# RWKV time mixing on one core: float32-word transpositions on TensorE between the matmuls of R, fewer units by the DMA crossbar

## The chip, the core and the metric

The kernel runs on one core of a Trainium2 chip. A core has TensorE (PE; its weight loads are listed as PEld), VectorE (DVE), ScalarE (ACT), GpSimd (POOL), SyncE (SP, which here only issues DMAs) and 16 DMA engines, each engine with a program of its own. The metric is the time of one execution on the device in microseconds (us), lower is better. The kernel before takes 199.12 us, the median of 3 runs (198.97 to 199.16).

## What is computed

`x` is 16 batches of 2048 tokens of 256 channels in float32. Each token is mixed with the one before it, multiplied by two 256 x 256 weights, gated, and multiplied by a third:

```python
x_prev[:, 1:, :] = x[:, :-1, :]          # zero for the first token
xv = x * time_mix_v + x_prev * (1 - time_mix_v)
xr = x * time_mix_r + x_prev * (1 - time_mix_r)
v = xv @ value_weight
r = xr @ receptance_weight
out = (1 / (1 + exp(-r)) * v) @ output_weight
```

(The reference also computes a `k`, which the output does not use.)

## The kernel before

**Tiles.** A unit is 512 tokens of one batch (`TU`), so there are 64 units, numbered `g` or `u`, four to a batch. TensorE needs the channels on the partitions, so each unit is transposed: tile `xt`, in two halves of 128 channels (`KO` = 2). The mix is written as xr = tm * (c * x_prev + x) with c = (1 - tm) / tm. The factor tm is multiplied into the weights once, at the start (`w_bf`), so a unit needs a scaling by `c_sb` (`scale`, `scale_pool` or `scale_act`, on DVE, POOL or ACT) and a sum (`add`, DVE), in tile `mix`.

**One step of the main loop** (over `g`) issues on TensorE: the four 512-column matmuls of R of unit g (`project`, into `psum_r`), the transpositions of a unit some six further on, the four matmuls of V of unit g (`psum_v`), and the eight 256-column matmuls of the output O of unit g - 1 (`out_matmuls`, `psum_o`). ACT takes the sigmoid of `psum_r` (`s_sb`), copies the transposed unit from PSUM (`ps_t`) to `xt`, and copies O to `o_sb`. DVE multiplies sigmoid and V (`z_sb`) and does the sums for the next units; POOL scales half of the pieces, each after a sum of DVE. From unit 10 on a piece for scaling holds two units. Which step scales and sums which unit is in the lists `products`, `sums`, `held` and `pooled`: the sum for R of unit g + 2 stands on DVE right behind z of step g.

**Two ways to transpose.** Units 0 to 39 (batches 0 to 9, `STAGED` = 10) are transposed by TensorE: x is loaded as bf16 (cast by the DMA), and eight 128 x 128 blocks are matmuls with x as the weights and the identity as the moving operand (`transposes`, `one`). Units 0 and 1, which come first, are loaded as float32 and transposed so. The last 24 units (batches 10 to 15) are cast into DRAM (`x_natural`) and brought in by two DMA transpositions through the crossbar (`by_dma`, issued by SP at steps 27 and 39, `T_AT`), three batches each. Steps from 34 on thus have no transpositions on TensorE; there ACT does some of the scaling (`FREE`), and O comes one step later (`LATE_O`).

**Queues.** SP issues the stores and the two crossbar transpositions in program order; stores of some steps are held back until a transposition has gone out (`FIRST`, `WAITING`). POOL issues the loads of x between its scalings (`LOADS` by unit to be transposed, `STAGE_AT` by step). A load for the second crossbar transposition waits in POOL's queue until the first has landed. The program order on every engine is written by hand, since the kernel schedules manually.

Names that the change touches: `transposes` and `one` (L254 on), `advance`, `project` (L384), `coefficients`, `first_transposes`, `scale`/`scale_pool`/`scale_act`, and the tables at the top. In the profile L272 is the transposition, L289 its copy by ACT, L384 the matmuls of R and V, L416 those of O, L376 the sums, L711 z, L672 the sigmoid, L364 the scaling by POOL, L254 the crossbar.

Of the kernel before, what the change touches and what calls it, by code (L numbers as in the profile page):

```python
# [1 line left out]

# [6 lines left out]
FP32 = mybir.dt.float32  # L9
# [6 lines left out]
def kernel(  # L16
# [39 lines left out]
    STAGED = 10  # L56
# [14 lines left out]
    SPARE = 9 * UB // 2  # L71
# [13 lines left out]
        (5, 0): (8, 10),  # L85
        (6, 0): (9,),
        (7, 0): (11,),
        (7, 1): (12,),
# [5 lines left out]
    xtpool = ctx.enter_context(tc.tile_pool(name="xtpool", bufs=2))  # L94
# [70 lines left out]
    tm_rows = consts.tile([2 * KO, P], FP32)  # L165
    w_f32 = consts.tile([P, 2, KO, D], FP32)
    for m, tm in enumerate([time_mix_r, time_mix_v]):
        nc.scalar.dma_start(
            out=tm_rows[m * KO : (m + 1) * KO, :], in_=tm.rearrange("(ko p) -> ko p", p=P)
        )  # L170

    def load_halves(e):
# [8 lines left out]
        out=w_f32[:, 0], in_=receptance_weight.rearrange("(ko p) n -> p ko n", p=P)  # L181
    )
    load_halves(1)
    nc.sync.dma_start(out=w_f32[:, 1], in_=value_weight.rearrange("(ko p) n -> p ko n", p=P))
# [47 lines left out]
    tm_prev = consts.tile([P, 2, KO], FP32)  # L232

    def coefficients():
        ps = ps_o_pool.tile([P, 2, KO], FP32, name="psum_o")
        nc.tensor.transpose(
            out=ps.rearrange("p m k -> p (m k)"), in_=tm_rows, identity=ident_f[: 2 * KO, : 2 * KO]
        )
# [21 lines left out]
    def transposes(i):  # L260

        b, e = divmod(i, UB)
        if b > 0 and e == 0:
            new_xt(b)
        if b >= BYUNIT:
            e = (e - 1) % UB
        j0 = 1 + e * UJ + (e if b < BYUNIT else 0)
        if b < BYUNIT or e == UB - 1:
            late_copies.append((b, e))

        def one(ps, jj, ko, src, idn):
            nc.tensor.transpose(  # L272
                out=ps[:, jj], in_=src[:, jj, ko * P : (ko + 1) * P], identity=idn
            )
# [14 lines left out]
        nc.scalar.copy(out=xt[b][:, j0 : j0 + UJ], in_=ps)  # L289
        if i in SHIFT_ACT:  # L290
            j, n = (j0 - 1, UJ) if b < BYUNIT else (0, J)
            nc.scalar.copy(out=xt[b][:, j, :, 1:P], in_=xt[b][:, j + n, :, 0 : P - 1])
            shifted.append((b, e))

    def first_transposes():
        def part(lo, n, pool, name):
            ps = pool.tile([P, n, KO, P], FP32, name=name)
            for jj in range(n):
                for ko in range(KO):
                    nc.tensor.transpose(  # L300
                        out=ps[:, jj, ko],
                        in_=x_unit[:, 0, lo + jj, ko * P : (ko + 1) * P],
                        identity=ident_f,
                    )
# [7 lines left out]
        part(1, 1, ps_o_pool, "psum_o")  # L312

# [48 lines left out]
    def scale_pool(piece, after):
        b, m, _, _ = piece
        op = nc.gpsimd.tensor_scalar(  # L364
            out=mixed(piece, 1),
            in0=tokens(piece, 0, 1),
            scalar1=c_sb[:, m, 1:2],
            scalar2=1.0,
            op0=ALU.mult,
            op1=ALU.mult,  # L370
        )
        tc.add_manual_dep(op.ins, after.ins.name, SYNC, reason="one at a time")
# [7 lines left out]
    def project(ps, g, m, lo=0, hi=TU):  # L380
        b, e = divmod(g, UB)
        for mo in range(KO):
            for ko in range(KO):
                nc.tensor.matmul(  # L384
                    out=ps[:, mo, :],
                    lhsT=w_bf[:, m, ko, mo * P : (mo + 1) * P],
# [3 lines left out]
                )  # L390

# [191 lines left out]
    first_transposes()  # L583
# [20 lines left out]
    )  # L604
    scale(pieces(0)[1])
# [43 lines left out]
    def scale_act(piece, kos):  # L649
        b, m, _, _ = piece  # L650
        for ko in kos:
# [4 lines left out]
                scale=c_sb[:, m, ko : ko + 1],  # L656
# [3 lines left out]
    for g in range(NU - 1):  # L660
        ps_r = ps_r_pool.tile([P, KO, TU], FP32, name="psum_r")
        if g == 0:
# [9 lines left out]
        nc.scalar.activation(out=s_sb, in_=ps_r, func=ACT.Sigmoid)  # L672
# [90 lines left out]
```

## Time and profile before

| | |
|---|---|
| median of 3 runs | 199.12 us |
| span of the profiled execution (first to last instruction) | 197.1 us |
| granted TensorE clock, mean | 0.999 |
| DMA traffic | 58.13 MB, 295 GB/s |
| HBM read, written | 34.34 MB, 39.90 MB |
| crossbar transpositions, issue to landing | 15.2 and 19.0 us |

How to read it: a group's row gives the line of the code, the engine, the operation, output and inputs, shape and count, then its busy time, the mean length of one in ns, and idle time of the engine ahead of it. A timeline row gives start and length in us, and in brackets how long the engine was idle before and what ended that. A row of a stretch (as 80.00:90.00) gives, in this order, the busy time of PE, PEld, DVE, ACT and POOL with counts, the granted clock, the DMA share and GB/s. Matmuls are pipelined: the next starts before the last has ended, so the step from start to start is what one costs.

### The profile page before, as it was taken

How to read it: one execution, taken by the hardware profiler on the slowest of the kernel's cores; microseconds unless marked ns; L12 is line 12 of the kernel's file. 1: busy time of each engine (PE TensorE's matmuls, PEld its weight loads, DVE VectorE, ACT ScalarE, POOL GpSimd, SP SyncE). 2: the span in 40 equal slices, each digit the busy share in tenths (PEclk: the TensorE clock that was granted, in tenths of full speed). 3: DMA queues.
4: the chain of work that ended last, by engine and by line, in shares of the span. 5: the costliest groups of instructions: out<-in, count | busy, mean ns of one | idle time of the engine just before them, and what ended most of it. 6: DMA issues, size and time to landing. Idle time of an engine off the chain costs nothing.

```text
span 197.1 us, 3735 instructions
## 1 busy us (share of the span) xinstructions
PE 191.8 (97%) x1358; PEld 123.3 (63%) x1364; DVE 183.2 (93%) x286; ACT 177.2 (90%) x197; POOL 85.9 (44%) x117
## 2 busy tenths in 40 slices
PE   8999999999999999999999999999999999999992
PEld 3556676666666666666666666666666666666660
DVE  0999999999999999999999999999999999999962
ACT  3799899999999999999999999999999999999982
POOL 2745542443665635624334266444443444444200
PEclk9999999999999999999999999999999999999999
DMA  5999999999999999999999999999999999999875
GB/s 171 244 190 223 218 263 253 248 264 259 300 419 278 289 294 336 271 236 206 367 206 290 330 347 191 204 210 284 290 301 424 421 419 419 411 422 421 338 321 219
DMA packets 35465, 58.13 MB, mean 295 GB/s; under 512 B 26004, under 2 KB 27000, under 8 KB 30712
## 3 DMA queue, kind: packets, MB, share of 16 engines
q1 hardware_dynamic: 31792, 41.34, 59.8%
q0 software_dynamic: 3504, 16.44, 41.6%
q8 instruction: 10, 0.16, 0.3%
q10 hardware_dynamic: 152, 0.13, 0.2%
q14 instruction: 7, 0.06, 0.1%
HBM read 34.34 MB, written 39.90 MB: 377 GB/s over the span
## 4 chain that ended last, share of the span: by engine, by line
PE 93%; DMA 4%; issue 0%; SPq 0%; ACT 0%
PE psum_r L384 28%; PE psum_v L384 27%; PE psum_o L416 27%; PE ps_t L272 9%; DMA x_bf<-in_x_dram 2%; DMA w_f<-n_receptance_weight_dram 2%; PE ps_t L416 1%; SPq L174 0%; PE psum_v L416 0%; PE ps_t L384 0%; PE psum_r L416 0%; ACT x_bf L446 0%
## 5 line engine op out<-in xcount | busy, mean ns | idle before, releaser
L364 POOL TENSOR_SCALAR mix<-xt_both,c_sb 128x1024 bf16<-128x1024 bf16 (+1 forms) x55 | 61.1, 1110 | 85.6 <-DVE mix L376 82.4
L711 DVE TENSOR_TENSOR z_sb<-s_sb,psum_v 128x1024 bf16<-128x1024 bf16 (+1 forms) x64 | 76.7, 1200 | 2.2 <-PE psum_v L384 1.1
L376 DVE TENSOR_TENSOR mix<-mix,xt_both 128x1024 bf16<-128x1024 bf16 x112 | 76.8, 696 | 1.4
L384 PEld LDWEIGHTS <-w_bf 128*128 128x128 bf16 x512 | 48.5, 98 | 39.1 <-DVE mix L376 0.4
L672 ACT ACTIVATE s_sb<-psum_r 128x1024 bf16<-128x1024 f32 x63 | 65.3, 1036 | 6.2 <-PE psum_r L384 6.0
L384 PE MATMUL psum_v<-mix,w_bf 128*128 128x512 bf16 (+1 forms) x252 | 64.8, 378 | 0.2
L384 PE MATMUL psum_r<-mix,w_bf 128*128 128x512 bf16 x250 | 64.6, 379 | 0.2
L416 PE MATMUL psum_o<-wo_bf,z_sb 128*128 128x256 bf16 x486 | 63.2, 273 | 0.0
L416 PEld LDWEIGHTS <-z_sb 128*128 128x128 bf16 x512 | 51.9, 103 | 17.9 <-DVE z_sb L510 0.7
L471 ACT COPY o_sb<-psum_o 128x1024 f32<-128x1024 f32 x50 | 51.2, 1024 | 4.9 <-PE psum_o L416 4.9
L289 ACT COPY xt_both<-ps_t 128x1024 bf16<-128x1024 bf16 x32 | 32.9, 1039 | 0.0
L272 PEld LDWEIGHTS <-x_bf 128*128 128x128 bf16 x304 | 19.7, 98 | 8.6 <-DMA x_bf<-in_x_dram 1.1
L272 PE MATMUL ps_t<-ident,x_bf 128*128 128x128 bf16 x304 | 22.5, 219 | 0.3 <-DMA x_bf<-in_x_dram 0.3
L354 DVE TENSOR_SCALAR mix<-xt_both,c_sb 128x1024 bf16<-128x1024 bf16 (+1 forms) x47 | 21.3, 463 | 0.0
L652 ACT ACTIVATE mix<-xt_both,c_sb 128x1024 bf16<-128x1024 bf16 x14 | 16.3, 1163 | 0.0
L376 DVE TENSOR_TENSOR mix<-mix,xt_first 128x1024 bf16<-128x1024 bf16 x15 | 10.6, 714 | 0.1
L471 ACT COPY x_bf<-psum_o 128x1024 f32<-128x1024 f32 x10 | 10.2, 1016 | 0.0
L354 DVE TENSOR_SCALAR mix<-xt_first,c_sb 128x512 bf16<-128x512 bf16 x22 | 6.6, 352 | 0.2
L289 ACT COPY xt_first<-ps_t 128x1024 bf16<-128x1024 bf16 x6 | 6.1, 1042 | 0.2 <-PE ps_t L272 0.2
L557 POOL COPY xt_first<-xt_first 128x254 bf16<-128x254 bf16 x5 | 2.0, 392 | 7.2 <-DVE mix L376 5.7
L364 POOL TENSOR_SCALAR mix<-xt_first,c_sb 128x512 bf16<-128x512 bf16 x6 | 4.1, 685 | 1.5 <-DVE mix L376 1.0
L162 POOL DMA_DIRECT2D x_bf<-in_x_dram x8 | 4.7, 583 | 0.0
(68 smaller groups left out, 52.6 us busy)
## 6 DMA issues: line engine op xcount, KB each, us to landing
out_dram<-o_sb SPq DMA_DIRECT2D x25, 1024.0 KB, 11.6
x_bf<-in_x_dram POOLq DMA_DIRECT2D x8, 1024.0 KB, 14.8
x_natural<-in_x_dram POOLq DMA_DIRECT2D x4, 1024.0 KB, 11.8
out_dram<-x_bf SPq DMA_DIRECT2D x4, 1024.0 KB, 14.4
x_natural<-in_x_dram POOLq DMA_DIRECT2D x4, 512.0 KB, 12.6
out_dram<-x_bf SPq DMA_DIRECT2D x4, 512.0 KB, 4.2
x_bf<-in_x_dram POOLq DMA_DIRECT2D x6, 256.0 KB, 6.5
o_sb<-in_x_dram SPq DMA_DIRECT2D x4, 256.0 KB, 3.8
```

What stands on the lines that cost most here:

```text
L162: return nc.gpsimd.dma_start(out=x_bf[b], in_=rows(b), max_dma_last_dim=run)
L272: nc.tensor.transpose(out=ps[:, jj], in_=src[:, jj, ko * P : (ko + 1) * P], identity=idn)
L289: nc.scalar.copy(out=xt[b][:, j0 : j0 + UJ], in_=ps)
L354: nc.vector.tensor_scalar(out=mixed(piece, ko), in0=tokens(piece, 0, ko), scalar1=c_sb[:, m, ko : ko + 1], scalar2=None, op0=ALU.mult,)
L364: op = nc.gpsimd.tensor_scalar(out=mixed(piece, 1), in0=tokens(piece, 0, 1), scalar1=c_sb[:, m, 1:2], scalar2=1.0, op0=ALU.mult, op1=ALU.mult,
L376: return nc.vector.tensor_tensor(out=mixed(piece), in0=mixed(piece), in1=tokens(piece, 1), op=ALU.add)
L384: nc.tensor.matmul(out=ps[:, mo, :], lhsT=w_bf[:, m, ko, mo * P : (mo + 1) * P], rhs=mixed((b, m, e * TU + lo, e * TU + hi), ko), start=(k ...
L416: nc.tensor.matmul(out=ps[:, j, :], lhsT=slot[:, ko, j], rhs=wo_bf[:, ko, :], start=(ko == 0), stop=(ko == KO - 1),)
L471: nc.scalar.copy(out=o[:, j0 : j0 + UJ, :], in_=ps)
L652: nc.scalar.activation(out=mixed(piece, ko), in_=tokens(piece, 0, ko), func=ACT.Copy, scale=c_sb[:, m, ko : ko + 1],)
L672: nc.scalar.activation(out=s_sb, in_=ps_r, func=ACT.Sigmoid)
L711: nc.vector.tensor_tensor(out=z_sb[:, :, c : c + n], in0=s_sb[:, :, c : c + n], in1=ps_v[:, :, c : c + n], op=ALU.mult,)
```

## The change

Four things change.

1. **Transpositions in float32 words.** A row of 256 bf16 channels is read as 128 words of float32, two neighbouring channels each. A unit takes four 128 x 128 float32 transpositions instead of eight of bf16, and ACT takes the two channels of each word apart when it copies (a step of two elements in PSUM). The halves `ko` of a unit transposed on TensorE thus hold the even and odd channels. Weights and coefficients for them are read in that order (`(p ko)` for `(ko p)`); units from the crossbar keep the old order, so a second set is made for them (`w_cross`, `c_cross`): two small transpositions at the start, a second load of both weights and a few operations at step 10 (`CROSS_AT`), four scalings by POOL at steps 20 to 23.
2. **Between the matmuls of R.** From step 3 on (`WEAVE`) the transpositions are issued one (or two, where a step has two units) behind each matmul of R, no longer all behind the fourth.
3. **16 units by the crossbar, not 24.** `STAGED` goes from 10 to 12: units 40 to 47 are transposed by TensorE, batches 12 to 15 come in two crossbar transpositions of two batches, at steps 32 and 41. The tables of loads, held stores and staging follow.
4. **Three tile buffers of two batches** (`xtpool`), instead of two of three.

```diff
-    STAGED = 10
+    STAGED = 12
-    T_AT = {27: 10, 39: 13}
-    FIRST = {19: 27, 21: 27, 27: 39}
-    WAITING = {23: 27, 25: 27, 29: 39, 31: 39, 33: 39, 35: 39}
+    T_AT = {32: 12, 41: 14}
+    FIRST = {23: 32, 25: 32, 33: 41}
+    WAITING = {27: 32, 29: 32, 35: 41, 37: 41}
+    CROSS_AT = 10
+    WEAVE = 3
-    STAGE_AT = {33: 13, 34: 14, 35: 15}
-    GROUPS = [(2, 3), (4, 5, 6), (7, 8, 9), (10, 11, 12), (13, 14, 15)]
-    HALVED = (12, 15)
+    STAGE_AT = {35: 14, 36: 15}
+    GROUPS = [(b, b + 1) for b in range(BYUNIT, B, 2)]
+    HALVED = (13, 15)
-        (5, 0): (8, 10),
+        (5, 0): (8,),
         (6, 0): (9,),
-        (7, 0): (11,),
-        (7, 1): (12,),
+        (7, 0): (10, 12),
+        (8, 0): (11,),
+        (8, 1): (13,),
-    xtpool = ctx.enter_context(tc.tile_pool(name="xtpool", bufs=2))
+    xtpool = ctx.enter_context(tc.tile_pool(name="xtpool", bufs=3))
...
-        out=w_f32[:, 0], in_=receptance_weight.rearrange("(ko p) n -> p ko n", p=P)
+        out=w_f32[:, 0], in_=receptance_weight.rearrange("(p ko) n -> p ko n", p=P)
...
+    def cross_coefficients():
+        nc.gpsimd.tensor_scalar(
+            out=tms_cross, in0=tm_cross, scalar1=0.0, scalar2=1e-30, op0=ALU.is_equal, op1=ALU.mult
+        )
+        nc.gpsimd.tensor_tensor(out=tms_cross, in0=tms_cross, in1=tm_cross, op=ALU.add)
+        nc.vector.reciprocal(c_cross, tms_cross)
+        nc.gpsimd.tensor_scalar(
+            out=c_cross, in0=c_cross, scalar1=-1.0, scalar2=1.0, op0=ALU.add, op1=ALU.mult
+        )
+
+    def load_cross_weights():
+        for m, w in enumerate([receptance_weight, value_weight]):
+            nc.gpsimd.dma_start(out=w_f32[:, m], in_=w.rearrange("(ko p) n -> p ko n", p=P))
...
-        ps = ps_t_pool.tile([P, UJ, KO, P], BF16, name="ps_t")
+        ps = ps_t_pool.tile([P, UJ, P], FP32, name="ps_t")
         src = x_first[:, e - 2] if b == 0 else x_bf[b][:, e * UJ : (e + 1) * UJ, :]
-        for jj in range(UJ):
-            for ko in range(KO):
-                one(ps[:, :, ko], jj, ko, src, ident)
-        nc.scalar.copy(out=xt[b][:, j0 : j0 + UJ], in_=ps)
+        words = src.bitcast(FP32)
+
+        def one(jj):
+            nc.tensor.transpose(out=ps[:, jj], in_=words[:, jj], identity=ident_f)
+
+        def evacuate():
+            nc.scalar.copy(
+                out=xt[b][:, j0 : j0 + UJ],
+                in_=ps.bitcast(BF16).rearrange("p j (c o) -> p j o c", o=KO),
+            )
...
-    def project(ps, g, m, lo=0, hi=TU):
+    def project(ps, g, m, lo=0, hi=TU, between=()):
         b, e = divmod(g, UB)
+        w = w_bf if b < STAGED else w_cross
+        between = list(between)
+        share = -(-len(between) // (KO * KO))
         for mo in range(KO):
             for ko in range(KO):
                 nc.tensor.matmul(
                     out=ps[:, mo, :],
-                    lhsT=w_bf[:, m, ko, mo * P : (mo + 1) * P],
+                    lhsT=w[:, m, ko, mo * P : (mo + 1) * P],
                     rhs=mixed((b, m, e * TU + lo, e * TU + hi), ko),
                     start=(ko == 0),
                     stop=(ko == KO - 1),
                 )
+                for one in between[:share]:
+                    one()
+                del between[:share]
...
+        limit = START_T[g] if g < len(START_T) else g + LOOK
+        between, ends = begin(limit) if g >= WEAVE else ([], [])
...
-            project(ps_r, g, 0)
+            project(ps_r, g, 0, between=between)
         s_sb = zpool.tile([P, KO, TU], BF16, name="s_sb")
         nc.scalar.activation(out=s_sb, in_=ps_r, func=ACT.Sigmoid)
-        advance(START_T[g] if g < len(START_T) else g + LOOK)
+        for end in ends:
+            end()
+        if g < WEAVE:
+            advance(limit)
...
+        if g == CROSS_AT:
+            load_cross_weights()
+            cross_coefficients()
+        if CROSS_AT + 10 <= g < CROSS_AT + 10 + 2 * KO:
+            scale_cross_weight(g - CROSS_AT - 10)
```

How this moves TensorE's instructions, at step 3, the first one that is woven. Of before, from the last matmul of R (`psum_r`) on, with the weight loads of each:

```order
L384 LDWEIGHTS w_bf
L384 MATMUL psum_r<-mix,w_bf 128x512
L272 LDWEIGHTS x_bf
L272 MATMUL ps_t<-ident,x_bf 128x128
L272 LDWEIGHTS x_bf
L272 MATMUL ps_t<-ident,x_bf 128x128
```

(six more such pairs follow, then V). Of the changed kernel, from the third matmul of R to the first of V; a float32 transposition stands as one instruction, which loads its weights itself:

```order
L436 LDWEIGHTS w_bf
L436 MATMUL psum_r<-mix,w_bf 128x512
L322 MATMUL ps_t<-ident_f,x_bf 128x128
L436 LDWEIGHTS w_bf
L436 MATMUL psum_r<-mix,w_bf 128x512
L322 MATMUL ps_t<-ident_f,x_bf 128x128
L436 LDWEIGHTS w_bf
L436 MATMUL psum_v<-mix,w_bf 128x512
```

Each transposition now stands between two matmuls of 512 columns.

At step 10 DVE's program of before reads, from z of that step to z of the next (`mix` is the pair of units 12 and 13, the sum behind z is the one for R of unit 12):

```order
L711 TENSOR_TENSOR z_sb_725<-s_sb_700,psum_v_720 128x1024
L376 TENSOR_TENSOR mix_182<-mix_182,xt_both_457 128x1024
L354 TENSOR_SCALAR mix_182<-xt_both_457,c_sb_134 128x8x128
L376 TENSOR_TENSOR mix_182<-mix_182,xt_both_457 128x1024
L711 TENSOR_TENSOR z_sb_764<-s_sb_745,psum_v_759 128x1024
```

In the changed kernel a reciprocal (L252) stands between z and the sum:

```order
L782 TENSOR_TENSOR z_sb_673<-s_sb_663,psum_v_668 128x1024
L252 RECIPROCAL c_cross_138<-tms_cross_137 128x4
L425 TENSOR_TENSOR mix_191<-mix_191,xt_both_436 128x1024
L403 TENSOR_SCALAR mix_191<-xt_both_436,c_sb_134 128x8x128
L425 TENSOR_TENSOR mix_191<-mix_191,xt_both_436 128x1024
L782 TENSOR_TENSOR z_sb_714<-s_sb_704,psum_v_709 128x1024
```

Its input comes from POOL, whose program at that place is, from the scaling of step 10 to those of the next two:

```order
L413 TENSOR_SCALAR mix_191<-xt_both_436,c_sb_134 128x8x128
L259 DMA w_f32_100<-in_receptance_weight_dram 128x2x256
L259 DMA w_f32_100<-in_value_weight_dram 128x2x256
L248 TENSOR_SCALAR tms_cross_137<-tm_cross_136 128x4
L251 TENSOR_TENSOR tms_cross_137<-tms_cross_137,tm_cross_136 128x4
L253 TENSOR_SCALAR c_cross_138<-c_cross_138 128x4
L413 TENSOR_SCALAR mix_192<-xt_both_436,c_sb_134 128x8x128 x2
```

So the reciprocal comes behind one scaling, two issued DMAs and two small operations of POOL.

More of the change, by code (lines that the diff above doesn't have):

```diff
@@ L1 @@
 from contextlib import ExitStack
+from functools import partial
 import concourse.bass as bass
@@ L164 @@
     x_unit = opool.tile([P, 2, UJ, D], FP32, name="o_sb")
-    tm_rows = consts.tile([2 * KO, P], FP32)
+    tm_rows = consts.tile([2, D], FP32)
     w_f32 = consts.tile([P, 2, KO, D], FP32)
     for m, tm in enumerate([time_mix_r, time_mix_v]):
-        nc.scalar.dma_start(
-            out=tm_rows[m * KO : (m + 1) * KO, :], in_=tm.rearrange("(ko p) -> ko p", p=P)
-        )
+        nc.scalar.dma_start(out=tm_rows[m : m + 1, :], in_=tm.rearrange("(o d) -> o d", o=1))
     def load_halves(e):
@@ L232, with mixes_by, scale_cross_weight @@
     tm_prev = consts.tile([P, 2, KO], FP32)
+    tm_cross = consts.tile([P, 2, KO], FP32)
+    tms_cross = consts.tile([P, 2, KO], FP32)
+    c_cross = consts.tile([P, 2, KO], FP32)
+    w_cross = consts.tile([P, 2, KO, D], BF16)
+    def mixes_by(order, pool, name):
+        ps = pool.tile([P, KO, 2], FP32, name=name)
+        rows = tm_rows.rearrange(order, k=KO)
+        for ko in range(KO):
+            nc.tensor.transpose(out=ps[:, ko], in_=rows[:, ko], identity=ident_f[:2, :2])
+        return ps.rearrange("p k m -> p m k")
+    def cross_coefficients():
[10 more added lines that the diff above has]
+            nc.gpsimd.dma_start(out=w_f32[:, m], in_=w.rearrange("(ko p) n -> p ko n", p=P))
+    def scale_cross_weight(n):
+        m, ko = divmod(n, KO)
+        nc.gpsimd.tensor_scalar(
+            out=halves(w_cross[:, m, ko, :]),
+            in0=apart(w_f32[:, m, ko, :]),
+            scalar1=tms_cross[:, m, ko : ko + 1],
+            scalar2=1.0,
+            op0=ALU.mult,
+            op1=ALU.mult,
+        )
     def coefficients():
[L235 to L238, printed above, removed]
+        ps = mixes_by("m (p k) -> m k p", ps_o_pool, "psum_o")
         tm = consts.tile([P, 2, KO], FP32)
@@ L269, in transposes @@
             late_copies.append((b, e))
[L271 to L274, printed above, removed]
         if i == 1:
@@ L278, in transposes, with channels @@
                 ps = ps_t_pool.tile([P, H, KO, P], FP32, name="ps_t")
+                src = channels(x_unit[:, i, h * H : (h + 1) * H])
                 for jj in range(H):
                     for ko in range(KO):
-                        one(ps[:, :, ko], jj, ko, x_unit[:, i, h * H : (h + 1) * H], ident_f)
+                        nc.tensor.transpose(
+                            out=ps[:, jj, ko], in_=src[:, jj, ko], identity=ident_f
+                        )
                 nc.scalar.copy(out=xt[b][:, j0 + h * H : j0 + (h + 1) * H], in_=ps)
-            return
-        ps = ps_t_pool.tile([P, UJ, KO, P], BF16, name="ps_t")
+            return [], None
+        ps = ps_t_pool.tile([P, UJ, P], FP32, name="ps_t")
         src = x_first[:, e - 2] if b == 0 else x_bf[b][:, e * UJ : (e + 1) * UJ, :]
-        for jj in range(UJ):
-            for ko in range(KO):
-                one(ps[:, :, ko], jj, ko, src, ident)
[L289 to L293, printed above, removed]
+        words = src.bitcast(FP32)
[5 more added lines that the diff above has]
+                in_=ps.bitcast(BF16).rearrange("p j (c o) -> p j o c", o=KO),
+            )
+            if i in SHIFT_ACT:
+                j, n = (j0 - 1, UJ) if b < BYUNIT else (0, J)
+                nc.scalar.copy(out=xt[b][:, j, :, 1:P], in_=xt[b][:, j + n, :, 0 : P - 1])
+                shifted.append((b, e))
+        return [partial(one, jj) for jj in range(UJ)], evacuate
+    def channels(t):
+        return t.rearrange("p j (c o) -> p j o c", o=KO)
     def first_transposes():
@@ L312, in first_transposes @@
         part(1, 1, ps_o_pool, "psum_o")
+        return mixes_by("m (k p) -> m k p", ps_t_pool, "ps_t")
     def slots(piece, off=0):
@@ L349, in mixed, with coefficient @@
         return cols if ko is None else cols[:, :, ko]
+    def coefficient(b, m, ko):
+        return (c_sb if b < STAGED else c_cross)[:, m, ko : ko + 1]
     def scale(piece, kos=(0, 1)):
@@ L356, in scale @@
                 in0=tokens(piece, 0, ko),
-                scalar1=c_sb[:, m, ko : ko + 1],
+                scalar1=coefficient(b, m, ko),
                 scalar2=None,
@@ L366, in scale_pool @@
             in0=tokens(piece, 0, 1),
-            scalar1=c_sb[:, m, 1:2],
+            scalar1=coefficient(b, m, 1),
             scalar2=1.0,
@@ L564, with begin @@
     tnext = 1
-    def advance(limit):
+    def begin(limit):
         nonlocal tnext
+        between, ends = [], []
         while tnext <= min(limit, NU - 1):
@@ L572, in advance @@
             if tnext < NU - BYDMA:
-                transposes(tnext)
+                ones, end = transposes(tnext)
+                between += ones
+                ends += [end] if end else []
             tnext += 1
+        return between, ends
+    def advance(limit):
+        between, ends = begin(limit)
+        for step in between + ends:
+            step()
     def apart(row):
@@ L604 @@
     )
+    nc.scalar.copy(out=tm_cross, in_=cross)
     scale(pieces(0)[1])
@@ L655, in scale_act @@
                 func=ACT.Copy,
-                scale=c_sb[:, m, ko : ko + 1],
+                scale=coefficient(b, m, ko),
             )
@@ L669 @@
         else:
-            project(ps_r, g, 0)
+            project(ps_r, g, 0, between=between)
         s_sb = zpool.tile([P, KO, TU], BF16, name="s_sb")
         nc.scalar.activation(out=s_sb, in_=ps_r, func=ACT.Sigmoid)
-        advance(START_T[g] if g < len(START_T) else g + LOOK)
+        for end in ends:
+            end()
+        if g < WEAVE:
+            advance(limit)
         if g in T_AT:
-            half, whole = loads[T_AT[g] + 2]
+            half, whole = loads[T_AT[g] + 1]
             for pair in firsts.pop(g):
```

8 lines of the change are left out of this document (4 added, 4 removed).

## The prediction

> **What bounds the kernel now.** I read the page's totals and its chain first, then TensorE's rows in order of time, then what the other engines have left in the same stretches.
>
> ```profile
> span 197.1 us, 3735 instructions
> PE 191.8 (97%) x1358; PEld 123.3 (63%) x1364; DVE 183.2 (93%) x286; ACT 177.2 (90%) x197; POOL 85.9 (44%) x117
> ...
> PE 93%; DMA 4%; issue 0%; SPq 0%; ACT 0%
> PE psum_r L384 28%; PE psum_v L384 27%; PE psum_o L416 27%; PE ps_t L272 9%; DMA x_bf<-in_x_dram 2%; DMA w_f<-n_receptance_weight_dram 2%; PE ps_t L416 1%; SPq L174 0%; PE psum_v L416 0%; PE ps_t L384 0%; PE psum_r L416 0%; ACT x_bf L446 0%
> ```
>
> TensorE is 93% of the chain that ended last, and the transpositions (L272) are 9% of it, some 17 us. A "busy" matmul row can hide gaps, so I checked the starts. Two steps of the main loop, first one with a transposition, then one whose unit comes by the crossbar (timeline, TensorE alone; start, length of the merged rows):
>
> ```profile
> 71.14 1.03 PE L384 MATMUL psum_r<-mix,w_bf 128*128 128x512 bf16 x4
> ...
> 72.00 0.61 PE L272 MATMUL ps_t<-ident,x_bf 128*128 128x128 bf16 x8
> ...
> 72.45 1.03 PE L384 MATMUL psum_v<-mix,w_bf 128*128 128x512 bf16 x4
> ...
> 73.31 1.04 PE L416 MATMUL psum_o<-wo_bf,z_sb 128*128 128x256 bf16 x8
> ...
> 74.19 1.03 PE L384 MATMUL psum_r<-mix,w_bf 128*128 128x512 bf16 x4
> ...
> 150.24 1.04 PE L416 MATMUL psum_o<-wo_bf,z_sb 128*128 128x256 bf16 x8
> ...
> 151.12 1.03 PE L384 MATMUL psum_v<-mix,w_bf 128*128 128x512 bf16 x4
> ...
> 152.84 1.04 PE L416 MATMUL psum_o<-wo_bf,z_sb 128*128 128x256 bf16 x8
> ```
>
> From R to R the first step is 74.19 - 71.14 = 3.05 us; its transpositions run from 72.00 to 72.45, so eight cost 0.45 us, 0.056 each. From O to O the crossbar step is 152.84 - 150.24 = 2.60 us: the same step without them. Matmuls follow each other at the rate of their columns in both, so TensorE is the bound, and any matmul time added to it is time of the kernel. The others have a little left: in 80 to 90 us DVE is busy 9.54 of 10 us and ACT 9.19, while TensorE is busy all ten.
>
> ```profile
> 80.00:90.00 10.00, 10.00 (x80) 6.58 (x78) 9.54 (x15) 9.19 (x11) 5.16 (x6) 1.00 1.03 246
> ```
>
> Where DMAs are nearly always busy (share 1.03 there) TensorE still does not wait for them, except once at the start. So the traffic that 8 fewer crossbar units save buys nothing by itself.
>
> **The transpositions: what one in float32 words costs.** The change replaces eight of bf16 by four of float32 for units 2 to 39, and adds four for each of units 40 to 47: 304 go (38 x 8), 184 come (46 x 4). The kernel before already transposes float32, for units 0 and 1, so a price is in the trace. Three rows of the groups, kept apart by shape (busy, mean ns of one):
>
> ```profile
> L416 PE MATMUL psum_o<-wo_bf,z_sb 128*128 128x256 bf16 x486 | 63.2, 273 | 0.0
> ...
> L272 PE MATMUL ps_t<-ident,x_bf 128*128 128x128 bf16 x304 | 22.5, 219 | 0.3 <-DMA x_bf<-in_x_dram 0.3
> ...
> L272 PE MATMUL ps_t<-ident_f,o_sb 128*128 128x128 f32 x8 | 1.0, 273 | 0.0
> ```
>
> A float32 transposition of 128 columns lasts 273 ns, like a bf16 matmul of 256 columns, not 219 like a bf16 one of 128. The starts agree (timeline, 5 to 14 us, then 7.9 to 8.1):
>
> ```profile
> 7.18 1.04 PE L272 MATMUL ps_t<-ident_f,o_sb 128*128 128x128 f32 x8
> 8.05 0.59 PE L398 MATMUL psum_r<-xt_first,w_prev 128*128 128x512 bf16 x2
> ...
> 7.72 0.49 PE L272 MATMUL ps_t<-ident_f,o_sb 128*128 128x128 f32 x3
> ...
> 7.94 0.21 PEld L398 LDWEIGHTS <-w_prev 128*128 128x128 bf16 x2
> ```
>
> Eight take 8.05 - 7.18 = 0.87 us, 0.109 each. The question is whether that is the pace of the stream or of the weight load in front of each, because between the matmuls of R a load has a 512-column matmul to hide behind. The last of the eight tells: behind it comes a bf16 load (7.94), which the bf16 transpositions show to fit into 0.056 us, and yet the next matmul starts only at 8.05. The last three take 0.33 us, 0.11 each, the last one too. So I take 0.109 us also for a woven one: 4 x 0.109 = 0.44 us for a unit against 0.45 before. Half as many instructions, the same time. Bounds: 0.109 above, 0.056 below.
>
> [...]
>
> Sum on TensorE: 184 x 0.109 = 20.1 us come, 304 x 0.056 = 17.0 us go: **+3.1 us**. Put by step: units 40 to 47 make eight steps 2.60 + 0.44 instead of 2.60 (+3.5), the others save a hundredth of a microsecond each (-0.4).
>
> **The new coefficients at step 10: a wait on DVE.** cross_coefficients puts a reciprocal on DVE between z of step 10 and the sum that R of step 12 needs, and it waits for POOL, which first scales a piece, issues two DMAs (the weights again) and does two tiny operations. The rows of before at that place (start, us):
>
> ```profile
> 42.01 0.58 POOL L162 DMA_DIRECT2D x_bf<-in_x_dram  x1
> ...
> 43.75 1.11 POOL L364 TENSOR_SCALAR mix<-xt_both,c_sb 128x1024 bf16<-128x1024 bf16 x1 [0.98 <-DVE mix L376]
> ...
> 46.77 1.03 PE L384 MATMUL psum_r<-mix,w_bf 128*128 128x512 bf16 x4
> ...
> 43.57 1.21 DVE L711 TENSOR_TENSOR z_sb<-s_sb,psum_v 128x1024 bf16<-128x1024 bf16 x1
> 44.70 0.70 DVE L376 TENSOR_TENSOR mix<-mix,xt_both 128x1024 bf16<-128x1024 bf16 x1
> ...
> L554 POOL COPY xt_first<-xt_first 128x2 bf16<-128x2 bf16 x5 | 1.6, 316 | 0.1
> ```
>
> POOL ends its scaling at 44.86, two issues of 0.58 bring it to 46.0, two operations of about 0.3 (the nearest row is the copy of 316 ns) to 46.6, and a reciprocal of 0.2 lets the sum start near 46.8 instead of 44.70. It ends at 47.5, and R of step 12, which started at 46.77, starts about 0.8 us late. Behind it in DVE's queue stand the scale and sum for V of step 12 and z of step 11, which O of step 11 waits for; by their lengths they come about 0.1 us late again. From there DVE gains 0.1 us a step (9.54 of 10) and catches up. The 2.1 us of DVE become **+0.9 us** on TensorE; bounds 0 (DVE further ahead by then) and 2.1 (nothing covered).
>
> **What I cost at nothing, and its cover.** Sigmoid waits for the last matmul of R, which woven transpositions delay by 3 x 0.109 = 0.33 us. ACT's rows of one step:
>
> ```profile
> 72.25 1.03 ACT L672 ACTIVATE s_sb<-psum_r 128x1024 bf16<-128x1024 f32 x1
> ...
> 73.17 1.02 ACT L289 COPY xt_both<-ps_t 128x1024 bf16<-128x1024 bf16 x1
> ...
> 73.58 1.22 DVE L711 TENSOR_TENSOR z_sb<-s_sb,psum_v 128x1024 bf16<-128x1024 bf16 x1 [0.22 <-PE psum_v L384]
> ...
> 74.39 1.01 ACT L471 COPY o_sb<-psum_o 128x1024 f32<-128x1024 f32 x1 [0.20 <-PE psum_o L416]
> ```
>
> Sigmoid then ends at 73.61 instead of 73.28, z starts about 0.1 us later and DVE's idle 0.22 takes that; ACT's own wait only moves from before the copy of O to before sigmoid. Early, ACT has nothing left:
>
> ```profile
> 30.00:40.00 10.00, 10.00 (x84) 6.69 (x82) 9.98 (x19) 10.00 (x12) 3.44 (x4) 1.00 1.04 258
> ```
>
> There the same delay can cost up to 0.5 us, but DVE (9.98 of 10) is as late, and its wait at step 10 covers what has piled up. The evacuation reads the same 1024 elements, now with a step of 4 bytes; copies of f32 from PSUM take 1.02 us like those of bf16, so no change. In units 40 to 47 half the scaling of V returns from ACT to DVE, where a step has 3.04 us again. Weaving needs x earlier by 0.65 us; its loads are issued four to twelve steps ahead. Three tile buffers relieve the first crossbar transposition of a wait, but nothing on TensorE waited for it. At the start the weights arrive in longer rows, two small transpositions stand before the coefficients, and TensorE's one wait is for x:
>
> ```profile
> 8.91 1.03 PE L384 MATMUL psum_v<-mix,w_bf 128*128 128x512 bf16 x4
> 10.25 0.62 PE L272 MATMUL ps_t<-ident,x_bf 128*128 128x128 bf16 x8 [0.31 <-DMA x_bf<-in_x_dram]
> ```
>
> V could have been followed at 8.91 + 0.87 = 9.78, so a faster weight load gains at most 0.5 us; the extra transpositions can lose 0.3. I take 0.
>
> **Sum.** 3.1 + 0.9 + 0 = 4.0 us on a span of 197.1 us, so 201.1. Around the span lie 2.0 us up to the median of the runs shown, 199.12; I add the same: **203.1 us**.
>
> **Rivals.** [...] Chance 0.08, two thirds of it for 198.3.
>
> *POOL waits for the crossbar.* The load of batch 14 stands in POOL's queue at step 35, three steps after the transposition it must wait for, where before there were six:
>
> ```profile
> 95.12 15.38 SPq L254 DMA_TRANSPOSE xt_both<-x_natural  x1
> ...
> xt_both<-x_natural SPq DMA_TRANSPOSE x2, 17.1
> ...
> 114.64 0.56 POOL L162 DMA_DIRECT2D x_natural<-in_x_dram  x1
> ...
> 107.70 1.03 PE L384 MATMUL psum_r<-mix,w_bf 128*128 128x512 bf16 x4
> ...
> 109.89 1.02 PE L384 MATMUL psum_r<-mix,w_bf 128*128 128x512 bf16 x4
> ```
>
> Three batches landed after 17.1 us, so two take about 11.4. The last two rows are R of steps 32 and 33. Before, step 33 reached its load at 114.64, 4.75 us after its R. Step 35 of the new kernel gets there near 107.70 + 0.9 + 3 x 3.04 + 4.75 = 122.5, so the transposition has to be issued by 111. Its batches are requested five steps before step 32 (107.7), as before, so it should be. If not, POOL, then DVE and TensorE are late by the excess; 2 us give 205.1. Chance 0.07.
>
> *The start or the early steps come out better:* x lands 0.5 us earlier and the wait at step 10 is covered: 203.1 - 0.5 - 0.9 = 201.7. It is the lower end of the forecast's own bounds.
>
> **How the numbers follow.** Forecast 0.82, first rival 0.08, second 0.07, others 0.03. The forecast's bounds are 201.7 (above) and 203.1 + 1.2 (nothing covered at step 10) + 0.5 + 0.3 = 205.1, which takes in the second rival; the first lies outside. Range 201.5 to 205.2. 0.2% (0.4 us) is about what a measurement of this kernel can tell from no change: slower 0.91, same 0.03, faster 0.06.
>
> **What would show it.** In the changed profile: 184 float32 transpositions of 273 ns; steps with them 3.04 us apart and R's 512-column matmuls 0.325 us apart within them; steps at 2.60 only from unit 48 on; DVE idle before L252 for about 1.7 us and R of the second step after it late. [...]

## The result and the profile after

The changed kernel takes **205.89 us**, the median of 4 runs (205.14 to 206.57), against 199.14 of the kernel before beside it: a ratio of 1.033 (95% interval 1.028 to 1.037), slower. The forecast was 203.1, with a range of 201.5 to 205.2.

The page of the changed kernel, totals and chain:

```profile
span 203.1 us, 3536 instructions
...
PE 196.3 (97%) x1247; PEld 130.2 (64%) x1247; DVE 186.6 (92%) x293; ACT 181.7 (89%) x202; POOL 91.1 (45%) x126
...
PE 86%; ACT 5%; DVE 4%; POOL 2%; issue 1%; POOLq 0%
```

TensorE's busy time grows by 4.5 us, and its share of the chain that ended last falls from 93% to 86%: ACT, DVE and POOL, which had no part in it worth a line, now hold 11%. That is the sign of waits on TensorE, beside more work. Where are they? I went through TensorE's starts in order and noted every step from start to start that is longer than its columns (0.216 us for 512, 0.109 for 256 or for a float32 transposition).

**The added work is what was forecast.** One woven step of the timeline, TensorE alone, and the group of the transpositions (kept apart by shape):

```profile
73.15 0.38 PE L436 MATMUL psum_r<-mix,w_bf 128*128 128x512 bf16 x1
73.37 0.27 PE L322 MATMUL ps_t<-ident_f,x_bf 128*128 128x128 f32 x1
73.48 0.38 PE L436 MATMUL psum_r<-mix,w_bf 128*128 128x512 bf16 x1
...
76.19 0.38 PE L436 MATMUL psum_r<-mix,w_bf 128*128 128x512 bf16 x1
```

```profile
L322 PE MATMUL ps_t<-ident_f,x_bf 128*128 128x128 f32 x184 | 46.5, 274 | 0.3 <-ACT xt_both L325 0.3
```

R's matmuls are 73.48 - 73.15 = 0.33 us apart: 0.216 for the 512 columns and 0.11 for the transposition. Its weight load stands beside R's matmul in time:

```profile
73.15 0.14 PEld L322 LDWEIGHTS ps_t<-ident_f,x_bf 128*128 128x128 f32 x1
```

It ends at 73.29, before the transposition starts at 73.37, and still the next matmul comes 0.11 us behind that start. So the 0.11 is not time of the load. The step takes 76.19 - 73.15 = 3.04 us. 184 transpositions at 0.109 are there, and the sum of all columns grows by 3.1 us.

**Waits at step 12.** TensorE, then DVE, then POOL in the timeline (in brackets the idle time before and what ended it):

```profile
46.26 1.04 PE L471 MATMUL psum_o<-wo_bf,z_sb 128*128 128x256 bf16 x8
47.91 0.39 PE L436 MATMUL psum_r<-mix,w_bf 128*128 128x512 bf16 x1 [0.61 <-DVE mix L425]
...
49.11 0.27 PE L322 MATMUL ps_t<-ident_f,x_bf 128*128 128x128 f32 x1
50.16 1.02 PE L436 MATMUL psum_v<-mix,w_bf 128*128 128x512 bf16 x4 [0.78 <-DVE z_sb L782]
```

```profile
47.09 0.18 DVE L252 RECIPROCAL c_cross<-tms_cross 128x4 f32<-128x4 f32 x1 [2.20 <-POOL tms_cross L251]
47.19 0.66 DVE L425 TENSOR_TENSOR mix<-mix,xt_both 128x1024 bf16<-128x1024 bf16 x1
...
48.89 1.22 DVE L782 TENSOR_TENSOR z_sb<-s_sb,psum_v 128x1024 bf16<-128x1024 bf16 x1
```

```profile
43.85 1.11 POOL L413 TENSOR_SCALAR mix<-xt_both,c_sb 128x1024 bf16<-128x1024 bf16 x1 [1.10 <-DVE mix L425]
44.92 0.79 POOL L259 DMA_DIRECT2D w_f<-n_receptance_weight_dram  x1
45.71 0.74 POOL L259 DMA_DIRECT2D w_f<-in_value_weight_dram  x1
46.53 0.24 POOL L248 TENSOR_SCALAR tms_cross<-tm_cross 128x4 f32<-128x4 f32 x1
46.86 0.20 POOL L251 TENSOR_TENSOR tms_cross<-tms_cross,tm_cross 128x4 f32<-128x4 f32 x1
```

DVE stands 2.20 us before the reciprocal. R of step 12 could have come at 46.26 + 0.87 = 47.13 and comes at 47.91, 0.78 late. V of step 12 could then have followed the last transposition at 49.11 + 0.11 = 49.22 and comes at 50.16, another 0.94 late, for z of step 11: there is one `psum_v`, and z must have read it (48.89 + 1.22 = 50.11) before V writes it again. Together **1.72 us**, where 0.9 was forecast.

**Waits where O begins to come a step later.** TensorE and ACT, at steps 40 to 42:

```profile
135.24 1.03 PE L436 MATMUL psum_v<-mix,w_bf 128*128 128x512 bf16 x4
136.40 0.38 PE L436 MATMUL psum_r<-mix,w_bf 128*128 128x512 bf16 x1
...
139.44 1.03 PE L436 MATMUL psum_r<-mix,w_bf 128*128 128x512 bf16 x4
140.69 1.03 PE L471 MATMUL psum_o<-wo_bf,z_sb 128*128 128x256 bf16 x8 [0.22 <-ACT o_sb L526]
```

```profile
135.33 1.02 ACT L740 ACTIVATE s_sb<-psum_r 128x1024 bf16<-128x1024 f32 x1 [0.18 <-PE psum_r L436]
...
139.61 1.03 ACT L526 COPY o_sb<-psum_o 128x1024 f32<-128x1024 f32 x1
```

Here no O stands between V of step 40 and R of step 41, so R would come at 135.24 + 0.86 = 136.10. But `psum_r` too is one buffer, and the sigmoid, which weaving has made late, reads it until 136.35: R starts 0.30 late. In step 42 O waits for ACT's copy of the O before it (140.64): 0.39 more. Together **0.69 us**; before, the same two places cost 0.06 (the trace has R of step 33 at 109.89, right behind V).

**An early wait.** TensorE at step 6, which has two units to transpose, and ACT:

```profile
28.23 0.38 PE L436 MATMUL psum_r<-mix,w_bf 128*128 128x512 bf16 x1
28.87 0.44 PE L322 MATMUL ps_t<-ident_f,x_bf 128*128 128x128 f32 x2 [0.26 <-ACT xt_both L325]
```

```profile
27.81 1.01 ACT L325 COPY xt_both<-ps_t 128x1024 bf16<-128x1024 bf16 x1
```

The third transposition is due behind the matmul, at 28.23 + 0.22 = 28.45, and needs a `ps_t` that ACT copies until 28.82: 0.42 late. All waits from 10 to 45 us add up to 1.6 us, 0.8 before.

**The sum.** From R of step 1 to the last two matmuls, first and last rows of TensorE's timeline of before and of after:

```profile
10.71 1.03 PE L384 MATMUL psum_r<-mix,w_bf 128*128 128x512 bf16 x4
...
192.94 0.39 PE L416 MATMUL psum_o<-wo_bf,z_sb 128*128 128x256 bf16 x2
```

```profile
10.37 1.03 PE L436 MATMUL psum_r<-mix,w_bf 128*128 128x512 bf16 x4
...
198.98 0.39 PE L471 MATMUL psum_o<-wo_bf,z_sb 128*128 128x256 bf16 x2
```

The stretch is 182.23 us before and 188.61 after, 6.38 longer: 3.1 of work, 1.7 at step 12, 0.6 at steps 41 and 42, 0.8 early. I use this stretch below beside the times, since what lies outside of it differs from execution to execution, as the last experiments show. It is read from one profiled execution each: a second one of the changed kernel, taken later, has 189.01, so a difference of 0.4 us in the stretch says nothing.

### The profile page after: what moved, and what is told of

It is laid out like the page before. It is cut to its first block, busy times and chain, and to the rows that moved or that the text cites. A ratio compares the mean times of both kernels' runs of the same rounds, so it can differ in the third digit from the quotient of the medians.

```text
span 203.1 us, 3536 instructions
## 1 busy us (share of the span) xinstructions
PE 196.3 (97%) x1247; PEld 130.2 (64%) x1247; DVE 186.6 (92%) x293; ACT 181.7 (89%) x202; POOL 91.1 (45%) x126
## 4 chain that ended last, share of the span: by engine, by line
PE 86%; ACT 5%; DVE 4%; POOL 2%; issue 1%; POOLq 0%
PE psum_v L436 24%; PE psum_o L471 24%; PE psum_r L436 24%; PE ps_t L322 8%; ACT s_sb L740 2%; PE ps_t L206 2%; DVE mix L425 2%; ACT xt_both L325 1%; DVE z_sb L782 1%; PE ps_t L471 1%; ACT o_sb L526 1%; POOL mix L413 1%; POOL w_f L259 1%; DVE mix L403 1%; ACT xt_first L315 1%
## 5 line engine op out<-in xcount | busy, mean ns | idle before, releaser
L413 POOL TENSOR_SCALAR mix<-xt_both,c_sb 128x1024 bf16<-128x1024 bf16 (+1 forms) x39 | 43.2, 1109 | 61.4 <-DVE mix L425 52.6
L436 PEld LDWEIGHTS <-w_bf 128*128 128x128 bf16 x380 | 37.0, 98 | 29.4 <-DVE mix L425 1.9
L436 PE MATMUL psum_v<-mix,w_bf 128*128 128x512 bf16 x192 | 49.3, 379 | 1.0 <-DVE z_sb L782 0.8
L322 PE MATMUL ps_t<-ident_f,x_bf 128*128 128x128 f32 x184 | 46.5, 274 | 0.3 <-ACT xt_both L325 0.3
L322 PEld LDWEIGHTS ps_t<-ident_f,x_bf 128*128 128x128 f32 x184 | 25.3, 141 | 5.4 <-ACT xt_both L325 1.4
L413 POOL TENSOR_SCALAR mix<-xt_both,c_cross 128x1024 bf16<-128x1024 bf16 x16 | 18.0, 1123 | 23.6 <-DVE mix L425 22.3
L436 PEld LDWEIGHTS <-w_cross 128*128 128x128 bf16 x132 | 12.9, 98 | 11.1
L436 PE MATMUL psum_r<-mix,w_cross 128*128 128x512 bf16 x64 | 16.4, 379 | 0.0
L436 PE MATMUL psum_v<-mix,w_cross 128*128 128x512 bf16 (+1 forms) x64 | 16.0, 372 | 0.0
L718 ACT ACTIVATE mix<-xt_both,c_cross 128x1024 bf16<-128x1024 bf16 x8 | 9.3, 1161 | 0.0
```

What stands on the lines that cost most here:

```text
L322: nc.tensor.transpose(out=ps[:, jj], in_=words[:, jj], identity=ident_f)
L413: op = nc.gpsimd.tensor_scalar(out=mixed(piece, 1), in0=tokens(piece, 0, 1), scalar1=coefficient(b, m, 1), scalar2=1.0, op0=ALU.mult, op1= ...
L436: nc.tensor.matmul(out=ps[:, mo, :], lhsT=w[:, m, ko, mo * P : (mo + 1) * P], rhs=mixed((b, m, e * TU + lo, e * TU + hi), ko), start=(ko = ...
L718: nc.scalar.activation(out=mixed(piece, ko), in_=tokens(piece, 0, ko), func=ACT.Copy, scale=coefficient(b, m, ko),)
```

## The experiments

The theory: beside the columns, the loss is the reciprocal behind POOL's two DMA issues (1.7), and the weaving, which makes the sigmoid late and wants `ps_t` early (0.3 to 1.0). The rival: the second weights, the permuted halves, the step of two elements in ACT's copy or the three buffers cost something wherever they stand.

### The reciprocal one step later, weaving off, and both

```diff
+    def cross_reciprocal():
         nc.vector.reciprocal(c_cross, tms_cross)
         nc.gpsimd.tensor_scalar(
...
             cross_coefficients()
+        if g == CROSS_AT + 1:
+            cross_reciprocal()
```

> The changed kernel, with the reciprocal of the crossbar coefficients (and the small POOL operation behind it) issued one step later, at step 11, when POOL's two operations ahead of it are long done. Theory (in the changed trace TensorE waits 0.78 us before R of step 12 for a sum of DVE and 0.94 us before V of step 12 for z of step 11, both behind that reciprocal): both waits go, 1.7 us less, about 204.2 us. Rival (DVE and ACT are so late there anyway that another wait takes their place): 205.4 us or more.

```diff
-    WEAVE = 3
+    WEAVE = 64
```

> The changed kernel with all transpositions behind the fourth matmul of R, as before the change (WEAVE out of reach); still four in float32 words a unit. Theory (a transposition costs 0.109 us wherever it stands, and weaving only makes it wait for ACT's copies early, 0.8 us, and sigmoid end later at steps 41 and 42, 0.7 us): 1.5 us less, about 204.4 us. Rival (between R's matmuls the weight loads hide and behind R they don't): 206 us or more.

Both edits together:

> Both edits together: reciprocal at step 11, no weaving. What is left of the change is float32 words, 16 units by the crossbar, three tile buffers, and the second weights. Theory: the two gains add, 205.9 - 1.7 - 1.5 = 202.7 us, which is the kernel before plus the 3.1 us of transpositions and a few tenths. Rival (they are one lateness, seen at two places): 203.8 us or more.

Measured, each 6 runs, beside 199.34 of the kernel before: **204.11** (ratio 1.024, 1.020 to 1.028), **205.06** (1.029, 1.025 to 1.033) and **202.87** (1.018, 1.015 to 1.022). The three theories' numbers hold to 0.1, 0.7 and 0.2 us. Without weaving alone less was won than expected, and TensorE's rows of that kernel say why:

```profile
46.47 1.04 PE L471 MATMUL psum_o<-wo_bf,z_sb 128*128 128x256 bf16 x8
48.38 1.04 PE L436 MATMUL psum_r<-mix,w_bf 128*128 128x512 bf16 x4 [0.88 <-DVE mix L425]
...
50.63 1.02 PE L436 MATMUL psum_v<-mix,w_bf 128*128 128x512 bf16 x4 [0.78 <-DVE z_sb L782]
```

R of step 12 now waits 48.38 - (46.47 + 0.87) = 1.04 us, for 0.78, and V 0.94 as before: together 1.98. What TensorE saves ahead of a wait is given to the wait. With the reciprocal moved the wait is gone (the stretch is 186.79 us, 1.82 shorter than that of the changed kernel), and both edits together come to 3.02 us under the changed kernel; the stretch of the third kernel is 185.86 us, 3.63 above before.

### The kernel before with 16 units by the crossbar

Only the tables of the third part of the change and the third buffer; bf16 transpositions, behind R, no second weights.

```diff
-    STAGED = 10
+    STAGED = 12
-    T_AT = {27: 10, 39: 13}
+    T_AT = {32: 12, 41: 14}
...
-    xtpool = ctx.enter_context(tc.tile_pool(name="xtpool", bufs=2))
+    xtpool = ctx.enter_context(tc.tile_pool(name="xtpool", bufs=3))
```

> The kernel before with only the tables of the change: 16 units by the crossbar, 48 by TensorE, three tile buffers of two batches; eight bf16 transpositions a unit, behind R. Theory (eight more units at 0.446 us on a TensorE that never waits): 199.1 + 3.6 = 202.7 us. Rival (less crossbar traffic frees the DMAs, which gives some of it back): under 202 us.

Measured: **202.70 us** (6 runs, 202.47 to 203.44; ratio 1.017, 1.014 to 1.020), 3.4 above before; the stretch is 186.08, 3.85 above. Eight units at 0.45 are 3.6. So with the same split between TensorE and crossbar the words cost what the bf16 blocks cost: 202.87 against 202.70, and the stretches stand the other way round by 0.22. Half as many instructions buy nothing that these runs can tell. Nor do the second weights, the permuted halves and ACT's copy in steps of two elements, which only the kernel of 202.87 has, cost anything that shows.

### The two calls of step 10 swapped

```diff
         if g == CROSS_AT:
-            load_cross_weights()
             cross_coefficients()
+            load_cross_weights()
```

> The changed kernel with only the two calls of step 10 in the other order: the small operations of POOL and the reciprocal first, the two loads of the second weights behind them. Theory (the wait of 1.72 us on TensorE at steps 10 and 11 comes from the reciprocal standing behind two DMA issues of 0.79 and 0.74 us): DVE's idle time before the reciprocal falls from 2.20 to about 0.7 us, V of step 12 and R of step 12 hardly wait, about 204.2 us, like the run that moved the reciprocal by a step (204.11). Rival (the wait is that of the extra operation on DVE, or of the extra traffic of the second weights, wherever it stands): about 205.9, like the changed kernel.

The profiled execution (204.05): DVE, then TensorE.

```profile
45.76 0.18 DVE L252 RECIPROCAL c_cross<-tms_cross 128x4 f32<-128x4 f32 x1 [0.71 <-POOL tms_cross L251]
...
47.56 1.22 DVE L782 TENSOR_TENSOR z_sb<-s_sb,psum_v 128x1024 bf16<-128x1024 bf16 x1
```

```profile
46.42 1.04 PE L471 MATMUL psum_o<-wo_bf,z_sb 128*128 128x256 bf16 x8
47.29 0.38 PE L436 MATMUL psum_r<-mix,w_bf 128*128 128x512 bf16 x1
...
48.48 0.27 PE L322 MATMUL ps_t<-ident_f,x_bf 128*128 128x128 f32 x1
48.82 1.02 PE L436 MATMUL psum_v<-mix,w_bf 128*128 128x512 bf16 x4
```

The same reciprocal and the same two loads, in the other order: DVE waits 0.71 us, not 2.20. R of step 12 follows O at once (46.42 + 0.87), and V, at 48.82 for 48.59, still comes right behind the end of z of step 11 (48.78). V of step 13 is 0.13 late. Of 1.72 us 0.36 are left: so 1.36 of the wait on TensorE comes from the two issues, and what is left goes through the one `psum_v`. The times did not say it so plainly: 203.89, 204.05, 207.07 and 207.45, so this kernel and the changed one were measured once more.

> The run with the two calls of step 10 swapped once more, since its four times fell into two pairs (203.89 and 204.05, 207.07 and 207.45) while its profile of 204.05 has 0.23 and 0.13 us of waits on TensorE at steps 10 to 12 for 0.78 and 0.94 of the changed kernel. Theory (the pair above is a disturbance at the start or the end of some executions, not of the order at step 10): most runs at 203.7 to 204.6, median about 204.1, 1.4 to 1.8 us under the changed kernel in the same call. Rival (the second weights, now issued behind the coefficients, hold POOL up in some executions): half of the runs again near 207.

> The changed kernel itself, beside the swapped one. Its profiled execution (205.14) is explained by waits on TensorE to 0.1 us, its median of four runs (205.89) is 0.7 us above that. If the 0.7 is a spread of the executions, more runs give a median of 205.1 to 205.6 with single ones above 206; if the profiled one was a lucky one and the waits at step 10 or at the early steps are often longer, the median stays at 205.9 and this profile shows waits of over 2 us at step 10 or over 1.9 us before it.

Swapped: **204.93** (6 runs, 204.24 to 206.36; ratio to before 1.029, 1.025 to 1.032); as it was: **205.64** (205.11 to 207.49; 1.033, 1.030 to 1.037). The profile of the changed kernel has the same 0.78 and 0.94 before R and V of step 12, that of the swapped one 0.24 before V of step 12 and 0.13 before V of step 13. By the stretch the order is worth 1.1 to 1.8 us (187.17 and 187.53 against 188.61 and 189.01), by the medians 0.7. Half of the swapped runs are where the theory had them (204.24 to 204.40), none is near 207, but the other half lies at 205.5 to 206.4, so the median of 204.1 that was expected did not come, and the difference of the medians is half of what was expected. The spans (first to last instruction) tell more than the times: four of the six swapped executions have 202.2 to 202.5 us, also the one of 205.46, and two have 204.2 and 204.5; those of the changed kernel are 203.1 to 205.3. By the medians of the spans (202.45 and 203.7) the order is worth 1.2 us. One of the two long swapped executions was profiled (206.24), and it is long at the start. Its TensorE, and then that of the changed kernel as first profiled:

```profile
7.04 1.06 PE L453 MATMUL psum_r<-xt_first,w_prev 128*128 128x512 bf16 x2
7.89 1.06 PE L453 MATMUL psum_r<-xt_first,w_bf 128*128 128x512 bf16 x2
...
10.30 0.59 PE L453 MATMUL psum_r<-xt_first,w_prev 128*128 128x512 bf16 x2
10.73 0.59 PE L453 MATMUL psum_r<-xt_first,w_bf 128*128 128x512 bf16 x2
```

```profile
7.99 0.59 PE L453 MATMUL psum_r<-xt_first,w_prev 128*128 128x512 bf16 x2
8.42 0.59 PE L453 MATMUL psum_r<-xt_first,w_bf 128*128 128x512 bf16 x2
```

At 7 us two matmuls of 512 columns take 0.85 us in the first, and 0.43 from 10.3 on: TensorE runs at half its pace until about 10 us. In the other execution the full pace is there from 3.9 us (float32 transpositions start 0.26 us apart at 3.61, 0.12 and 0.11 from 3.86 on). R of step 1 starts at 12.52 in the one and at 10.37 in the other, so about 2 us of a time have nothing to do with the program's order. The full pace came 6 us later in the one than in the other, and what delayed it is not shown. The start can be long for another reason too. In the profiled execution of the run with the reciprocal later (204.79) the full pace comes early (two matmuls of 512 columns take 0.43 us from 7.99 on), but TensorE waits for a load of x, and R of step 1 starts at 11.98:

```profile
11.51 0.63 PE L324 MATMUL ps_t<-ident_f,x_bf 128*128 128x128 f32 x4 [1.63 <-DMA x_bf<-in_x_dram]
```

Of the two runs of 207 no profile was taken, so what made them long stays open.

### Weaving only between the two ends

The reciprocal later, and the weaving at steps 12 to 38 alone (the expectation says 40; `LATE_O` is 40, so the condition ends at 38):

```diff
-        between, ends = begin(limit) if g >= WEAVE else ([], [])
+        between, ends = begin(limit) if 12 <= g < LATE_O - 1 else ([], [])
...
-        if g < WEAVE:
+        if not 12 <= g < LATE_O - 1:
             advance(limit)
```

> The changed kernel with the reciprocal a step later and the weaving only at steps 12 to 40, so neither at the early steps, where ACT has nothing left, nor at the step where O begins to come later. Theory (weaving costs only at these two ends): 202.8 us, like the run with no weaving at all (202.87). Rival (weaving costs something in the steps between too, spread thin): nearer to the fully woven one, 203.6 to 204.1.

Measured: **202.78 us** (4 runs, 202.72 to 203.04; ratio 1.017, 1.013 to 1.022), like the run with none (202.87) and 1.3 under the fully woven one (204.11). The 27 woven steps cost nothing that shows (the stretch is 185.98 us, with none woven 185.86); what the weaving costs lies at the two ends.

### Weaving alone, in bf16

The kernel before with its eight bf16 transpositions two by two behind the matmuls of R from step 3 on:

```diff
-            project(ps_r, g, 0)
+            project(ps_r, g, 0, between=between)
...
-        advance(START_T[g] if g < len(START_T) else g + LOOK)
+        for end in ends:
+            end()
+        if g < 3:
+            advance(limit)
```

> The kernel before with its bf16 transpositions, two behind each matmul of R from step 3 on; nothing else is changed. Theory (weaving delays the sigmoid and costs where ACT has nothing left, whatever the form of the transposition): slower by 0.7 to 1.2 us, 199.9 to 200.5. Rival one (only float32 transpositions, with their longer self-loads, lose by being woven): 199.2. Rival two (weight loads of the transpositions hide better between 512-column matmuls): faster than 198.7.

Measured: **200.37 us** (12 runs, 199.97 to 201.51) against 199.11; ratio 1.005 (1.003 to 1.008); the stretch is 1.37 longer. TensorE, at step 6, and at steps 32 to 34, where this kernel's O becomes later:

```profile
28.56 0.38 PE L390 MATMUL psum_r<-mix,w_bf 128*128 128x512 bf16 x1
29.25 0.38 PE L273 MATMUL ps_t<-ident,x_bf 128*128 128x128 bf16 x4 [0.31 <-ACT xt_both L289]
...
109.70 1.03 PE L390 MATMUL psum_v<-mix,w_bf 128*128 128x512 bf16 x4
110.86 0.38 PE L390 MATMUL psum_r<-mix,w_bf 128*128 128x512 bf16 x1
...
113.90 1.03 PE L390 MATMUL psum_r<-mix,w_bf 128*128 128x512 bf16 x4
115.15 1.03 PE L425 MATMUL psum_o<-wo_bf,z_sb 128*128 128x256 bf16 x8 [0.22 <-ACT o_sb L480]
```

The same three waits at the same places, 0.47, 0.30 and 0.38 us. So they belong to the weaving, not to float32, and a bf16 transposition does not get cheaper between R's matmuls either: R's starts at 74.87 and 75.20 are 0.33 us apart with two between them, so 0.11 for the two.

### Words with the tables of before

The changed kernel with 24 units by the crossbar, two buffers, no weaving and the reciprocal later:

```diff
-    STAGED = 12
+    STAGED = 10
...
-    WEAVE = 3
+    WEAVE = 64
...
+        if g == CROSS_AT + 1:
+            cross_reciprocal()
```

> The changed kernel's float32 words, second weights and coefficients, with the tables of before: 24 units by the crossbar, two tile buffers, no weaving, the reciprocal a step later. Theory (the loss is the 8 units moved to TensorE, the weaving at both ends and the wait at step 10): 38 units at 0.437 for 0.446 us gain 0.3 to 0.4 us, so 198.8 to 199.4, same as before or just faster. Rival (the second weights, the permuted halves or the copy with a step of two elements cost something of their own): 199.9 or more, and waits for ACT's copies on TensorE.

Measured: **201.08 us** (12 runs, 199.46 to 202.63) against 199.11; ratio 1.010 (1.007 to 1.013). By its time the rival has it; its stretch is 182.58 us, 0.35 longer than before, which is within what two executions of one kernel differ by. The columns are down by 0.37 as expected, but 0.30 of waits appear before V of steps 46 and 47 (units by the crossbar) and some at the first steps. Most of the rest of the profiled execution (200.15) is behind the last matmul: SP's last store takes 3.6 us from issue to landing, 2.1 before. The span ends 5.3 us behind the start of the last matmul row, 4.2 in before. It could be the 0.5 MB more that the second weights bring to DMA engines which are busy nearly to the end here (58.64 MB for 58.13, share 0.99 from 185 to 190 us); but the run without weaving and with the reciprocal later has the same long landing (3.6) with its DMA engines at half load from 170 to 185 us (share 0.51 to 0.53). This stays open, and so does why the median lies 0.9 above the profiled execution. With 24 units the rival is thus not ruled out. In any case no kernel of this study beats the one before.

## Why the prediction missed

**The work: right.** 184 transpositions of 0.109 came and 304 of 0.056 went, +3.1; 8 units in bf16 measured +3.4 to +3.9. A float32 transposition of 128 columns took as long as a bf16 matmul of 256, 0.109 us from start to start, also where its load is hidden. The first rival, with the chance of 0.08 and two thirds of it for 198.3 us, put a float32 transposition between R's matmuls at 0.056 us, so R's starts 0.216 + 0.056 = 0.27 us apart. No run shows that price: the starts are 0.33 apart, and the float32 transposition takes 0.109 us, twice the 0.056 of the bf16 one. One line of the forecast was misplaced: steps of 2.60 begin behind step 42, not 48, since transpositions run six units ahead; their number is the same.

**The wait at step 10: right mechanism, half the size.** +0.9 was forecast, 1.72 measured. R of step 12 was late by 0.78, forecast 0.8. The step that failed is "by their lengths they come about 0.1 us late again", and with it that only O of step 11 waits for z. V of step 12 comes before that O, in the one `psum_v`. The rows were there in the profile of before, z of step 11 on DVE and V of step 12 on TensorE:

```profile
46.52 1.21 DVE L711 TENSOR_TENSOR z_sb<-s_sb,psum_v 128x1024 bf16<-128x1024 bf16 x1
```

```profile
48.08 1.03 PE L384 MATMUL psum_v<-mix,w_bf 128*128 128x512 bf16 x4
```

z ends at 47.73, so V had 0.35 us to spare, where R had 46.77 - 45.40 = 1.37. A delay of DVE is paid at the consumer with the least slack: z of step 11 came 48.89 - 46.52 = 2.37 us later, of which TensorE was late already by 0.36 (O of step 11 at 46.26, for 45.90), and 2.01 less 0.35 is 1.66, near the 1.72 measured. The two issues, taken at 0.58 each, took 0.79 and 0.74, which made it longer by 0.4.

**Weaving at nothing: wrong.** It was checked in a step from the middle, and there it is free, as the run that weaves only there shows. For the early steps up to 0.5 us was allowed, as a bound and by way of a late sigmoid; the steps where O begins to come later were not looked at. It costs at step 6 (0.42, `ps_t`) and at steps 41 and 42 (0.63, `psum_r` and `psum_o`), about 1 us in all; the bf16 kernel shows it by itself, +1.26. "Its wait at step 10 covers what has piled up" was half right: without weaving that wait grew by 0.26.

**The other rivals.** POOL did wait for the crossbar, as the second rival had it:

```profile
123.77 0.57 POOL L166 DMA_DIRECT2D x_natural<-in_x_dram  x1 [1.27 <-DMA xt_both<-x_natural]
```

Two batches landed 15.5 us after their issue at 107.74, not 11.4, and POOL's load went out at 123.77. It cost nothing: TensorE's starts from 118 to 134 us follow each other by their columns, since POOL waits for DVE before its scalings anyway, 2.09 us just before (at 121.37). An earlier start gave nothing to count on.

**The rest.** 3.1 + 1.7 + 0.6 + 0.8 = 6.2 of the 6.4 us; the early 0.8 is 0.4 of weaving and some small waits, for x and for mixes, that were not taken apart. The profiled execution (205.14) is the fastest of four, and the median lies 0.75 above it; what the others lost was not seen. The second profiled execution (205.99) shows the kind of it: its stretch is 0.40 longer, by waits before 16 us, and behind the stretch it takes 4.8 us for 4.1, with SP's last store landing in 2.9 us for 2.0. Not tried: a second `psum_v`.

## What to carry to other kernels

When an edit makes an engine late, list all that stands behind it in the queue, and for each the next consumer and its slack; price the delay by the smallest slack, and count the single PSUM buffer that must be read before it is written again among the consumers. An edit that is free in the middle of a loop is still to be checked where the order changes: at the first steps, and where a stage begins to come later. And half the instructions are no gain where each takes twice as long: a unit's four float32 transpositions took 0.44 us here, its eight in bf16 0.45.

## What the hardware showed that was not expected

- A float32 transposition took 0.109 us from its start to that of the next matmul even with its load hidden, for 171 of the 184; a bf16 one took 0.056.
- Issuing one DMA of a 256 KB weight took POOL 0.73 to 0.83 us in the runs that do it, where eight loads of x in the kernel before took 0.58 on the mean.
- The moment at which TensorE reaches its full pace differed by 6 us between two executions of nearly the same program (3.9 and 10.1 us), which moved R of step 1 by 2.15 us; the granted clock is 1.00 in every stretch of the first 12 us in both, so it does not show this.
- SP's last store took 2.0 to 2.1 us to land in nine of the twelve profiled executions, 2.9 in one and 3.6 in two, which moves the end by over 1 us.
